# Retention heads of a decoder trunk: the transposes of a head in one row, and query and key products over two banks

## The chip, the cores and the metric

The kernel runs on one core of a Trainium2 chip. The metric is the device time of one execution in microseconds, as the median of several executions. Beside it stands one profiled execution, from which all durations in this document come. Engines are named as in the profile: PE is TensorE (PEld its weight loads), DVE is VectorE, ACT is ScalarE, POOL is GpSimd, SP issues the DMAs.

## The reference

A decoder trunk of two layers, 256 tokens, model width 2048, in float32. Layer 0 mixes tokens by retention, layer 1 by a short gated convolution, and each is followed by a SwiGLU feed-forward stage. The change touches the retention layer alone:

```python
def retention_mixer(h, cos, sin, w_in, w_out):
    q, k, v, g = jnp.split(h @ w_in, [qk_w, 2 * qk_w, 2 * qk_w + v_w], axis=-1)
    q = rope(split_heads(q, RET_HEADS), cos, sin)
    k = rope(split_heads(k, RET_HEADS), cos, sin) * (RET_DK ** -0.5)
    v = split_heads(v, RET_HEADS)
    ...
    o = rms_norm(chunked_gated_linear_attention(q, k, v, log_a))
    o = merge_heads(o).astype(h.dtype)
    return ((jax.nn.silu(g) * o) @ w_out).astype(h.dtype)
```

There are 8 heads; a head has 256 query and key columns and 512 value and gate columns.

## The kernel before, in words

**Products in two parts.** Activations and weights are held as a high part (`hi`, float32r) and a rest (`lo`). A product of a 128x128 weight block with all 256 tokens is hi·h_hi + hi·h_lo + lo·h_hi. There are two ways to write it. `packed` issues three matmuls of 256 columns, all adding into one half of a PSUM bank (L397, L398, L399), so that two blocks of output columns share a bank. `product`, which the feed-forward stages and the output projections use, issues one matmul of 512 columns, whose moving operand is both parts of h and whose results fill a bank (L357), and one of 256 columns for lo, into the second half (L360); its two halves are added later (`summed`: ScalarE copies one, VectorE adds the other, L407 and L409). A value or gate product of width 512 goes by `by_token` (L372 to L374): the tokens are the stationary operand, and a block of 512 columns takes six matmuls. PSUM has eight banks, all from one pool, which hands a bank on when its last reader is through.

**Weights.** They come by DMA in 1 MB tiles in the order of use. Each half of a tile is prepared, two halves ahead, by ScalarE (`hi`, L312) and VectorE (`lo`, L315); a half holds 8 blocks of 128 columns. VectorE also reduces modulation weights (L246) at a lower priority.

**Order.** The instructions of TensorE stand in the order in which the program writes them. Those of VectorE and ScalarE in the heads' stage are ordered by a scheduler's priorities.

**The retention layer.** An opening stage computes, for some heads, the query, key and gate products over part of the 16 rows of weights, and holds the sums in SBUF (`ahead`). Then the heads follow in the order 4, 0, 2, 1, an output projection for these four, 5, 3, 6, 7, and the second output projection. The rows left for the head's own products are none for head 4, four for heads 0 and 1, eight for 2 and 3, and sixteen for 5, 6 and 7. `projections` writes a head as: query product and `rope`, key product and `rope`, value product, scores, gate product. With two blocks of columns each for query and key, all heads together have 2 x 2 x (2 x 4 + 2 x 8 + 3 x 16) = 288 such blocks.

**What a head leaves to the next.** `mixed` returns three steps, which run between the matmuls of whatever follows, after 8, 8 and 20 ticks (a tick is a block of 128 columns): the outputs of the first 128 tokens, those of the second with the norm and the gate (L878, giving the two tiles `o`), and `ends`. `ends` transposes `o` (two tiles of 128x512) into four pieces of 128x256 with eight transposes (L890) and splits each piece into its high and low part, `mid` (L414 on ScalarE, L415 on VectorE). Two pieces share a bank. The program's dependencies go by bank: a write to a bank waits for the reads of it that the program wrote before. `mid` is what the output projection reads; the four pieces of the latest head come last in it.

Of the kernel before, what the change touches and what calls it, by code (L numbers as in the profile page):

```python
# [14 lines left out]
ALU = mybir.AluOpType  # L15
PSUM = bass.MemoryType.PSUM

P = 128
D = 2048
S = 256  # L20
# [105 lines left out]
RET_SPANS, RET_HEADS = ret_in_groups()  # L126
# [61 lines left out]
def trunk(ctx: ExitStack, tc: tile.TileContext, x_in, c_in, pos_in, w_mod, cols_in, tab_in, w_all, out):  # L188
    nc = tc.nc
# [7 lines left out]
    def name(s):  # L197
        serial[0] += 1
        return f"{s}_{serial[0]}"

    def tmp(tag, shape=(P, S), dtype=F32, pool=work, bufs=None):
        return pool.tile(list(shape), dtype, tag=tag, name=name(tag), bufs=bufs)
# [24 lines left out]
    inv_freq, ident = tab[:, 0:1], tab[:, 1 : 1 + P]  # L227
# [107 lines left out]
    def bank():  # L335
        return ps.tile([P, 2, S], F32, tag="bank", name=name("bank"))
# [10 lines left out]
    def product(g, act, base=0, before=None, banks=None, last=True):  # L347

        fresh = not banks
        banks = banks or [bank() for _ in g.cols]  # L350
        for k in g.ks:
            if before:
                before(k)
            h = act[k - base]
            for c, pt in zip(g.cols, banks):
                hi, lo = take(g, k, c)
                nc.tensor.matmul(  # L357
                    pt, hi, h, start=fresh and k == g.ks[0], stop=False, skip_group_check=True
                )
                nc.tensor.matmul(  # L360
                    pt[:, 1, :], lo, h[:, 0, :], start=False, stop=last and k == g.ks[-1], skip_group_check=True
                )
            ticked(len(g.cols))
        paced(len(g.cols) * len(g.ks))
        return banks
# [10 lines left out]
    def packed(g, act, base=0, before=None, between=None, banks=None):  # L376

        banks = banks or [bank() for _ in range((g.n + 1) // 2)]
        for k in g.ks:
            if before:
                before(k)
            h = act[k - base]
            at = 0
            for i, (c, width) in enumerate(g.items):
                if between and i == len(g.items) // 2:
                    between(k)
                hi, lo = take(g, k, c, width)  # L390
                if width == DV:
                    by_token(banks[at // 2 : at // 2 + 2], hi, lo, h, k == g.ks[0], k == g.ks[-1])
                    at += 4
                    continue
                pt = banks[at // 2][:, at % 2, :]
                first, last = k == g.ks[0] and at % 2 == 0, k == g.ks[-1]
                nc.tensor.matmul(pt, hi, h[:, 0, :], start=first, stop=False, skip_group_check=True)  # L397
                nc.tensor.matmul(pt, hi, h[:, 1, :], start=False, stop=False, skip_group_check=True)  # L398
                nc.tensor.matmul(pt, lo, h[:, 0, :], start=False, stop=last, skip_group_check=True)  # L399
                at += 1  # L400
            ticked(g.n)
        paced(g.n * len(g.ks))
        return banks

    def summed(pt, dst=None, at=slice(0, S)):
        low = tmp("low", bufs=3)
        nc.scalar.copy(low[:, at], pt[:, 1, at])  # L407
        dst = tmp("sum", bufs=4) if dst is None else dst
        nc.vector.tensor_tensor(dst, pt[:, 0, at], low[:, at], op=ALU.add)  # L409
        return dst  # L410

    def split(dst, src, at=slice(0, S)):

        nc.scalar.copy(dst[:, 0, at], src)  # L414
        nc.vector.tensor_tensor(dst[:, 1, at], src, dst[:, 0, at].bitcast(F32), op=ALU.subtract)  # L415
# [66 lines left out]
    h = [h_all[:, j, :, :S] for j in range(KT)]  # L482
# [83 lines left out]
    with ExitStack() as inner:  # L566
# [48 lines left out]
        ahead = {}  # L615

        free, tag_of = [f"mid{n}" for n in range(20)], {}
# [13 lines left out]
        with tc.tile_pool(name="start", bufs=1) as sp:  # L631
# [59 lines left out]
            with tc.manual_schedule(engines={mybir.EngineType.DVE, mybir.EngineType.Activation}):  # L691
# [16 lines left out]
                for i in range(0, D, 2 * S):  # L708
                    pt = bank().rearrange("p a b -> p (a b)")
# [24 lines left out]
                pt = norm_sums([acc[0][:, 0, :]])  # L734
# [16 lines left out]
                banks = [bank() for _ in range(8)]  # L751
# [48 lines left out]
        mid = [None] * (4 * HEADS)  # L800

        rp = inner.enter_context(tc.tile_pool(name="rpool", bufs=1))

        def rope(s, tag):
            a = tmp("qa", (P, 2, S), pool=rp, bufs=1)
            nc.vector.tensor_tensor(a, s, cos.unsqueeze(1).to_broadcast([P, 2, S]), op=ALU.mult)
            b = tmp("qb", (P, 2, S), pool=rp, bufs=1)
            nc.vector.tensor_tensor(b[:, 0, :], s[:, 1, :], sin, op=ALU.mult)
            nc.vector.tensor_tensor(b[:, 1, :], s[:, 0, :], sin, op=ALU.mult)
            nc.vector.tensor_tensor(a[:, 0, :], a[:, 0, :], b[:, 0, :], op=ALU.subtract)  # L810
            nc.vector.tensor_tensor(a[:, 1, :], a[:, 1, :], b[:, 1, :], op=ALU.add)
            dst = rp.tile([P, 2, 2, S], F32R, tag=tag, name=name(tag))
            nc.scalar.copy(dst[:, 0, :, :], a)
            nc.vector.tensor_tensor(dst[:, 1, :, :], a, dst[:, 0, :, :].bitcast(F32), op=ALU.subtract)
            return dst

        def gate(s):

            g = rp.tile([P, 2, S], F32, tag="sg", name=name("sg"), bufs=2)
            nc.scalar.activation(g, s, AF.Silu)  # L820
            return g.rearrange("p a b -> p (a b)")
# [34 lines left out]
        def mixed(head, both, v, sg):  # L856

            total = tmp("osum", (P, 2), bufs=2)
            pts, os = [], []

            def outputs(t):

                pt = bank().rearrange("p a b -> p (a b)")
                pts.append(pt)
                n = 0
                for jt in range(t + 1):
                    sp = both[jt][:, :, (t - jt) * P : (t - jt + 1) * P]
                    for i, j in ((0, 0), (0, 1), (1, 0)):
                        nc.tensor.matmul(pt, sp[:, i, :], v[:, jt, j, :], start=n == 0, stop=n == 3 * t + 2)
                        n += 1  # L870
                sq = rp.tile([P, DV], F32, tag="o", name=name("sq"), bufs=2)
                nc.scalar.activation(sq, pt, AF.Square, accum_out=total[:, t : t + 1])

            def normed_outputs():
                r = roots_of(total, DV)
                for t, pt in enumerate(pts):
                    o = rp.tile([P, DV], F32, tag="o", name=name("o"), bufs=2)
                    nc.vector.scalar_tensor_tensor(o, pt, r[:, t : t + 1], sg[t], op0=ALU.mult, op1=ALU.mult)  # L878
                    os.append(o)

            def last_outputs():
                outputs(1)
                normed_outputs()

            def ends():
                for i in range(4):
                    if i % 2 == 0:
                        pt = bank()
                    for t, o in enumerate(os):
                        nc.tensor.transpose(  # L890
                            pt[:, i % 2, t * P : (t + 1) * P], o[:, i * P : (i + 1) * P], ident
                        )
                    n = 4 * head + i
                    mid[n] = rm_tile(("mid", n), F32R)
                    split(mid[n], pt[:, i % 2, :])

            return list(zip(STEPS, [lambda: outputs(0), last_outputs, ends]))

        def pair(head, i):

            g = RET_HEADS[head][0][i]
            if not g.ks:
                return [ahead[head, n] for n in ((i,) if i < 2 else (2, 3))]
            sums = packed(g, h)
            for j, pt in enumerate(sums):
                key = (head, i + j)
                if key in tag_of:
                    free.append(tag_of.pop(key))
                if key in ahead:
                    s = tmp("qs", (P, 2, S), pool=rp, bufs=1)  # L910
                    nc.vector.tensor_tensor(s, ahead[key], pt, op=ALU.add)
                    sums[j] = s
            return sums

        def projections(head):
            q = rope(*pair(head, 0), "q")
            k = rope(*pair(head, 1), "k")
            v = values(head, RET_HEADS[head][1])
            sp = scores(head, q, k)
            sg = [gate(s) for s in pair(head, 2)]  # L920
            asides.extend(mixed(head, sp, v, sg))
            since[0] = 0

# [45 lines left out]
    mid = [mpool.tile([P, 2, S], F32R, tag=f"mid{i}", name=name("mid")) for i in range(KT)]  # L969
    pending, done = [], 0  # L970
    for i, g in enumerate(CONV_IN):
        pending += [sums(g)] if i else normed(acc, 1, 0, g)
        while len(pending) >= 3:
            pb, pc, pu = pending[:3]
            pending = pending[3:]
            j = done
# [74 lines left out]
```

## Time and the profile before

| | us |
|---|---|
| median of three executions | 2684.3 (2682.7 to 2688.4) |
| the profiled execution, its own time | 2684.1 |
| its span, from the first to the last instruction | 2682.3 |
| heads' stage with both output projections | about 195 to 825 of the span |

A row of the waits list reads: engine, tile and line that waited, what ended the wait, then total us, number of waits, the longest. A row of the table by windows gives, for one stretch, the busy time of each engine in us with its instructions, the granted TensorE clock as a share of full speed (PEclk), the busy share of the DMA engines and GB/s. In the timeline a row is one or several equal instructions with start and duration in us; matmuls overlap, so the spacing of their starts, not the duration, is what one costs.

### The profile page before, as it was taken

Reading aid. Unit: us, or ns where it says so; the run is one execution under the profiler, and the core shown is the slowest. Engines: PE = TensorE matmul, PEld = TensorE weight load, DVE = VectorE, ACT = ScalarE, POOL = GpSimd, SP = SyncE. Lnnn points to the kernel's source line nnn. Section 1 sums busy time; section 2 is a strip of 40 time slices with the busy share of each in tenths; the row PEclk is TensorE's granted clock in tenths of the full one; section 3 lists DMA queues with packets and bytes.
Section 4 is the critical chain, followed back from the end, with each engine's and each line's share of the span. In section 5 each row is a group of like instructions: output and inputs, shape, how many; then the busy total and the mean of one; then the engine's idle time right before and its main releaser. Section 6 shows DMA issues by size and latency. Waiting matters only on the chain.

```text
span 2682.3 us, 38239 instructions
## 1 busy us (share of the span) xinstructions
PE 2627.3 (98%) x15220; PEld 2303.8 (86%) x15220; DVE 1993.6 (74%) x2543; ACT 1248.4 (47%) x1770; POOL 145.8 (5%) x230
## 2 busy tenths in 40 slices
PE   7999899999999999999999999999999999999998
PEld 6988789878889888888888898888998888888887
DVE  7997768777678887777777879888886765555564
ACT  5644443444446454334444454444554443444443
POOL 0000000100000001100000001100000000000000
PEclk9999999999999999999999999999999999999999
DMA  9966558866767887777777768776767665555553
GB/s 398 388 269 242 222 192 313 295 226 253 250 223 254 301 307 282 272 279 282 282 273 276 276 221 313 297 281 247 280 252 266 256 230 188 189 189 189 189 189 126
DMA packets 96950, 687.58 MB, mean 256 GB/s; under 512 B 10753, under 2 KB 12545, under 8 KB 13825
## 3 DMA queue, kind: packets, MB, share of 16 engines
q1 hardware_dynamic: 96770, 685.13, 68.8%
q8 instruction: 119, 1.95, 0.3%
q14 instruction: 61, 0.50, 0.0%
HBM read 682.99 MB, written 2.10 MB: 255 GB/s over the span
## 4 chain that ended last, share of the span: by engine, by line
PE 73%; issue 19%; DVE 4%; DMA 2%; ACT 1%; POOL 0%; DVEq 0%; ACTq 0%; POOLq 0%
PE bank L357 34%; PE bank L360 17%; PE bank L372 4%; PE bank L373 4%; PE bank L374 4%; PE bank L399 2%; PE bank L397 2%; PE bank L398 2%; PE bank L517 1%; PE bank L516 1%; PE bank L518 1%; DVE lo L315 1%; DMA raw<-w_all 1%; DVE raw L642 1%; DMA raw<-w_mod 1%
## 5 line engine op out<-in xcount | busy, mean ns | idle before, releaser
L315 DVE TENSOR_TENSOR lo<-raw,hi 128x1024 fp32r<-128x1024 f32 x912 | 1113.5, 1224 | 583.2 <-ACT hi L312 581.1
L312 ACT CAST hi<-raw 128x1024 fp32r<-128x1024 f32 x912 | 955.1, 1052 | 1118.4 <-PE bank L357 644.3
L357 PE MATMUL bank<-h,hi 128*128 128x512 f32 x3296 | 1155.3, 395 | 0.0
L360 PE MATMUL bank<-h,lo 128*128 128x256 f32 x3296 | 924.4, 280 | 0.0
L357 PEld LDWEIGHTS bank<-h,hi 128*128 128x128 f32 x3296 | 622.5, 189 | 145.3
L360 PEld LDWEIGHTS bank<-h,lo 128*128 128x128 f32 x3296 | 622.0, 189 | 0.0
L357 PE MATMUL bank<-mid,hi 128*128 128x512 f32 x1604 | 556.3, 393 | 0.0
L360 PE MATMUL bank<-mid,lo 128*128 128x256 f32 x1604 | 444.9, 277 | 0.1
L246 DVE SCALAR_TENSOR_TENSOR raw<-raw,cb 128x2048 f32<-128x2048 f32 x160 | 365.8, 2286 | 13.7 <-DMA raw<-w_mod 13.5
L357 PEld LDWEIGHTS bank<-mid,hi 128*128 128x128 f32 x1604 | 300.7, 187 | 69.4
L360 PEld LDWEIGHTS bank<-mid,lo 128*128 128x128 f32 x1604 | 301.3, 188 | 0.5 <-DVE lo L315 0.5
L372 PE MATMUL bank<-hi,h 128*128 128x512 f32 x512 | 206.1, 403 | 0.0
L373 PE MATMUL bank<-lo,h 128*128 128x512 f32 x512 | 205.3, 401 | 0.0
L374 PE MATMUL bank<-hi,h 128*128 128x512 f32 x512 | 205.0, 400 | 0.0
L357 PE MATMUL bank<-rm,hi 128*128 128x512 f32 x496 | 177.2, 401 | 0.0
L399 PE MATMUL bank<-h,lo 128*128 128x256 f32 x512 | 147.1, 287 | 6.8 <-DVE lo L315 6.8
L397 PE MATMUL bank<-h,hi 128*128 128x256 f32 x512 | 146.9, 287 | 2.5 <-ACT h L670 2.5
L398 PE MATMUL bank<-h,hi 128*128 128x256 f32 x512 | 146.5, 286 | 0.5 <-DVE h L671 0.5
L360 PE MATMUL bank<-rm,lo 128*128 128x256 f32 x496 | 139.9, 282 | 0.0
L374 PEld LDWEIGHTS bank<-hi,h 128*128 128x128 f32 x512 | 98.4, 192 | 23.4
L372 PEld LDWEIGHTS bank<-hi,h 128*128 128x128 f32 x512 | 98.7, 193 | 20.2
L373 PEld LDWEIGHTS bank<-lo,h 128*128 128x128 f32 x512 | 98.3, 192 | 20.1
(152 smaller groups left out, 2255.3 us busy)
## 6 DMA issues: line engine op xcount, KB each, us to landing
raw<-w_all SPq DMA_DIRECT2D x456, 1024.0 KB, 4.9
raw<-w_mod SPq DMA_DIRECT2D x192, 1024.0 KB, 5.0
x<-x_in SPq DMA_DIRECT2D x4, 512.0 KB, 5.6
out<-out SPq DMA_DIRECT2D x5, 256.0 KB, 2.9
decay<-tab_in SPq DMA_DIRECT2D x8, 128.0 KB, 2.1
out<-out SPq DMA_DIRECT2D x3, 128.0 KB, 2.3
out<-out SPq DMA_DIRECT2D x1, 384.0 KB, 2.7
cols<-cols_in SPq DMA_DIRECT2D x1, 160.0 KB, 8.7
```

Source lines behind the costliest of these rows:

```text
L246: nc.vector.scalar_tensor_tensor(raw, raw, 1.0, cb, op0=ALU.mult, op1=ALU.mult, accum_out=total)
L312: nc.scalar.copy(hi, raw)
L315: nc.vector.tensor_tensor(lo, raw, hi.bitcast(F32), op=ALU.subtract)
L357: nc.tensor.matmul(pt, hi, h, start=fresh and k == g.ks[0], stop=False, skip_group_check=True)
L360: nc.tensor.matmul(pt[:, 1, :], lo, h[:, 0, :], start=False, stop=last and k == g.ks[-1], skip_group_check=True)
L372: nc.tensor.matmul(o, ht[:, 0, :], hi, start=first, stop=False)
L373: nc.tensor.matmul(o, ht[:, 0, :], lo, start=False, stop=False)
L374: nc.tensor.matmul(o, ht[:, 1, :], hi, start=False, stop=last)
L397: nc.tensor.matmul(pt, hi, h[:, 0, :], start=first, stop=False, skip_group_check=True)
L398: nc.tensor.matmul(pt, hi, h[:, 1, :], start=False, stop=False, skip_group_check=True)
L399: nc.tensor.matmul(pt, lo, h[:, 0, :], start=False, stop=last, skip_group_check=True)
L516: nc.tensor.matmul(pt, hi, rows[0], start=k == 0, stop=False)
```

## The change

`ends` takes both banks first, issues the eight transposes in one row, tile by tile of `o`, and then the four splits. The query and key products of a head go through `product` instead of `packed`: a product holds two banks instead of one. Where a partial sum is held, VectorE adds it to the first halves of both banks and then adds the second halves, four operations of 256 columns in place of one of 512; where none is held, `summed` puts the sums into SBUF, and `rope` reads them there instead of from the bank. For head 4, which has no rows left, nothing changes in the products. The gates keep `packed`, in a function of their own.

```diff
             def ends():
+                turned = [bank() for _ in range(2)]
+                for t, o in enumerate(os):
+                    for i in range(4):
+                        nc.tensor.transpose(
+                            turned[i // 2][:, i % 2, t * P : (t + 1) * P], o[:, i * P : (i + 1) * P], ident
+                        )
                 for i in range(4):
-                    if i % 2 == 0:
-                        pt = bank()
-                    for t, o in enumerate(os):
-                        nc.tensor.transpose(
-                            pt[:, i % 2, t * P : (t + 1) * P], o[:, i * P : (i + 1) * P], ident
-                        )
                     n = 4 * head + i
                     mid[n] = rm_tile(("mid", n), F32R)
-                    split(mid[n], pt[:, i % 2, :])
+                    split(mid[n], turned[i // 2][:, i % 2, :])
...
         def pair(head, i):
 
             g = RET_HEADS[head][0][i]
+            key = head, i
             if not g.ks:
-                return [ahead[head, n] for n in ((i,) if i < 2 else (2, 3))]
-            sums = packed(g, h)
-            for j, pt in enumerate(sums):
-                key = (head, i + j)
-                if key in tag_of:
+                return ahead[key]
+            banks = product(g, h)
+            s = tmp("qs", (P, 2, S), pool=rp, bufs=1)
+            if key in ahead:
+                free.append(tag_of.pop(key))
+                for n, pt in enumerate(banks):
+                    nc.vector.tensor_tensor(s[:, n, :], ahead[key][:, n, :], pt[:, 0, :], op=ALU.add)
+                for n, pt in enumerate(banks):
+                    nc.vector.tensor_tensor(s[:, n, :], s[:, n, :], pt[:, 1, :], op=ALU.add)
+            else:
+                for n, pt in enumerate(banks):
+                    summed(pt, s[:, n, :])
+            return s
...
         def projections(head):
-            q = rope(*pair(head, 0), "q")
-            k = rope(*pair(head, 1), "k")
+            q = rope(pair(head, 0), "q")
+            k = rope(pair(head, 1), "k")
             v = values(head, RET_HEADS[head][1])
             sp = scores(head, q, k)
-            sg = [gate(s) for s in pair(head, 2)]
+            sg = gates(head)
```

More of the change, by code (lines that the diff above doesn't have):

```diff
@@ L901, in pair, with gates @@
             g = RET_HEADS[head][0][i]
+            key = head, i
             if not g.ks:
-                return [ahead[head, n] for n in ((i,) if i < 2 else (2, 3))]
-            sums = packed(g, h)
-            for j, pt in enumerate(sums):
-                key = (head, i + j)
-                if key in tag_of:
+                return ahead[key]
[11 more added lines that the diff above has]
+            return s
+        def gates(head):
+            g = RET_HEADS[head][0][2]
+            if not g.ks:
+                return [gate(ahead[head, n]) for n in (2, 3)]
+            sg = []
+            for t, pt in enumerate(packed(g, h)):
+                key = (head, 2 + t)
+                if key in ahead:
                     free.append(tag_of.pop(key))
-                if key in ahead:
                     s = tmp("qs", (P, 2, S), pool=rp, bufs=1)
                     nc.vector.tensor_tensor(s, ahead[key], pt, op=ALU.add)
-                    sums[j] = s
-            return sums
+                    pt = s
+                sg.append(gate(pt))
+            return sg
         def projections(head):
-            q = rope(*pair(head, 0), "q")
-            k = rope(*pair(head, 1), "k")
+            q = rope(pair(head, 0), "q")
+            k = rope(pair(head, 1), "k")
             v = values(head, RET_HEADS[head][1])
             sp = scores(head, q, k)
-            sg = [gate(s) for s in pair(head, 2)]
+            sg = gates(head)
             asides.extend(mixed(head, sp, v, sg))
```

## The prediction

> **What bounds the kernel now.** I read the page first, then the waits of the matmul engine, then its timeline around one place, then stretches in the table by windows.
>
> ```profile
> span 2682.3 us, 38239 instructions
> PE 2627.3 (98%) x15220; PEld 2303.8 (86%) x15220; DVE 1993.6 (74%) x2543; ACT 1248.4 (47%) x1770; POOL 145.8 (5%) x230
> ```
>
> TensorE (PE) is busy 98% of the span, so the time is the length of its instruction stream plus its waits. Its own waits:
>
> ```profile
> PE bank L890 <- DVE rm L415: 26.3, 16, 2.5
> PE bank L399 <- DVE lo L315: 6.8, 6, 2.3
> ```
>
> The first row is by far the largest: 26.3 us in 16 waits, all before a transpose (L890) and all ended by VectorE's half of a split (L415). Eight heads give 16, two for each head. The second row lies in the opening stage, which the change leaves alone. One head's transposes, as TensorE ran them:
>
> ```profile
> 229.81 0.39 PE L373 MATMUL bank<-lo,h 128*128 128x512 f32 x1
> 230.04 0.39 PE L374 MATMUL bank<-hi,h 128*128 128x512 f32 x1
> 230.27 0.38 PE L890 MATMUL bank<-tab,o 128*128 128x128 f32 x2
> 232.50 0.66 PE L890 MATMUL bank<-tab,o 128*128 128x128 f32 x4 [1.85 <-DVE rm L415]
> 234.30 0.69 PE L890 MATMUL bank<-tab,o 128*128 128x128 f32 x2 [1.14 <-DVE rm L415]
> 234.64 0.78 PE L372 MATMUL bank<-hi,h 128*128 128x512 f32 x1
> 235.21 0.63 PE L373 MATMUL bank<-lo,h 128*128 128x512 f32 x1
> 235.64 0.63 PE L374 MATMUL bank<-hi,h 128*128 128x512 f32 x1
> 236.06 0.63 PE L372 MATMUL bank<-hi,h 128*128 128x512 f32 x1
> 236.49 0.63 PE L373 MATMUL bank<-lo,h 128*128 128x512 f32 x1
> 236.92 0.63 PE L374 MATMUL bank<-hi,h 128*128 128x512 f32 x1
> ```
>
> Columns are start, duration, engine, line, operands, and the idle time before. Two transposes run, the next two wait 1.85 us because they write the bank that the split of the first two is still reading, then four run (the third pair is in a fresh bank), and the last two wait 1.14 us for the split of the third pair. Behind them the 512-column matmuls start 0.43 us apart (235.64, 236.06, 236.49, 236.92), where before the transposes they started 0.23 us apart (229.81, 230.04). So the wait has a second price, the granted clock:
>
> ```profile
> core 0: us, PE busy (x) PEld busy (x) DVE busy (x) ACT busy (x) POOL busy (x), PEclk, DMA share, GB/s
> 234.04:237.45 3.41, 3.15 (x9) 2.57 (x10) 0.63 (x2) 0.37 (x1) 0.00 (x0) 0.50 0.82 271
> ...
> 752.86:756.27 3.41, 3.41 (x13) 2.82 (x12) 1.68 (x2) 0.10 (x1) 0.00 (x0) 0.50 0.40 166
> sum 27.28, PE 26.16 PEld 22.55 DVE 15.47 ACT 4.77 POOL 0.69; mean PE 3.27 PEld 2.82 DVE 1.93 ACT 0.60 POOL 0.09
> ```
>
> These are eight stretches of 3.41 us, one behind each head's transposes, all at a clock of 0.50, with 26.16 us of busy TensorE in them. What brings such a stretch is seen in the ones just ahead, cut at the same 3.41 us steps:
>
> ```profile
> 36.07:39.48 3.41, 3.41 (x23) 3.07 (x21) 3.41 (x3) 0.17 (x1) 0.00 (x0) 1.00 1.00 408
> 32.66:36.07 3.41, 2.26 (x16) 2.06 (x16) 3.03 (x4) 3.38 (x6) 0.00 (x0) 1.00 1.01 418
> 152.12:155.53 3.41, 1.49 (x12) 1.48 (x12) 3.41 (x6) 3.21 (x5) 0.00 (x0) 1.00 0.10 38
> 155.53:158.94 3.41, 3.41 (x12) 2.86 (x11) 3.41 (x4) 1.05 (x2) 0.00 (x0) 0.50 0.95 387
> 230.63:234.04 3.41, 0.68 (x5) 0.42 (x4) 3.41 (x6) 1.31 (x4) 0.00 (x0) 1.00 0.01 2
> ```
>
> After 2.26 us busy out of 3.41 the next stretch keeps the full clock; after 1.49 (no transposes in it) and after 0.68 (transposes) the next has half. The point lies between 1.49 and 2.26.
>
> **The change part by part. First, the transposes in a row.** Both banks are taken before the first transpose and all four pieces of a bank are written before its split starts, so neither of the two waits has anything left to wait for: 26.3 us go. A wait also breaks the overlap of neighbours:
>
> ```profile
> L890 PEld LDWEIGHTS bank<-tab,o x64: 137/141/226, 230.0 to 752.2; 128*128 128x128 f32 x64
> L890 PE MATMUL bank<-tab,o x64: 270/272/476, 230.3 to 752.3; 128*128 128x128 f32 x64
> ```
>
> A transpose lasts 0.272 us alone but follows its neighbour after one weight load, 0.141 us, so each of the 16 waits costs another 0.131 us that its idle column does not show: 2.1 us. Sum 28.4 us. Check on the head shown: 234.64 − 230.27 = 4.37 us, less 8 × 0.141 = 1.13, is 3.24; its two waits give 1.85 + 1.14 + 2 × 0.131 = 3.25.
>
> The four splits (eight instructions, as before) now follow with no transpose queued behind them. Only the output projection reads their results, and that comes after four heads; the last head of each four has its transposes inside that projection, whose own rows for this head are kept for last. So they cost TensorE nothing while VectorE finds the time.
>
> **Second, the clock.** With the stalls gone a 3.41 us stretch holds 1.13 us of transposes and matmuls otherwise, so it is busy throughout. A 512-column matmul takes 0.233 us at the full clock and 0.427 at half; the 26.16 busy us shrink by 1 − 0.233/0.427 = 0.454, which is 11.9 us. Bounds: 0, if something else keeps the clock low, and 8 × 3.41 × 0.454 = 12.4.
>
> On this the Trainium skill speaks against the change: "TensorE: Matmul & The Clock Gate", Part 4, says that transpose-mode work does not count as busy for the clock. By it the eight transposes would be 1.13 us of idle to the clock, which alone leaves 2.28 counted; no run here has transposes back to back, so the trace neither bears it out nor refutes it. The sum by the rule is the same unless another wait comes beside them (a rival below).
>
> **Third, query and key products.** Three 256-column matmuls for a weight block (L397 to L399) become one of 512 and one of 256 columns (L357, L360): the same 768 columns, one instruction and one weight load less. Rates from long stretches, by starts:
>
> ```profile
> 453.83 0.28 PE L397 MATMUL bank<-h,hi 128*128 128x256 f32 x1
> ...
> 476.67 0.39 PE L372 MATMUL bank<-hi,h 128*128 128x512 f32 x1
> ```
> ```profile
> 366.94 0.39 PE L357 MATMUL bank<-rm,hi 128*128 128x512 f32 x1
> ...
> 375.41 0.38 PE L890 MATMUL bank<-tab,o 128*128 128x128 f32 x2
> ```
>
> The first is head 5's 64 blocks: 22.84/64 = 0.357 us. The second is 24 blocks of an output projection: 8.47/24 = 0.353. A row of the groups from 195 to 770 us counts the blocks:
>
> ```profile
> L397 PE MATMUL bank<-h,hi 128*128 128x256 f32 x288 | 82.5, 286 | 0.0
> ```
>
> 288 × 0.004 = 1.2 us saved; bounds 0 and 2.4. The durations (three of 0.286 against 0.40 + 0.28) promise far more, but matmuls overlap and only starts count.
>
> **Fourth, VectorE has more to do.** Four heads add their held partial sums: one 512-column add (0.68 us) for each product becomes four of 256. Three heads fed rope from the bank: now ScalarE copies two 256-column halves and VectorE adds two. What these cost:
>
> ```profile
> L911 DVE TENSOR_TENSOR qs<-rm,bank 128x512 f32<-128x512 f32 x16 | 10.9, 682 | 0.8 <-PE bank L399 0.8
> L407 ACT COPY low<-bank 128x256 f32<-128x256 f32 x8 | 3.1, 382 | 0.1
> 229.61 0.42 DVE L810 TENSOR_TENSOR qa<-qa,qb 128x256 f32<-128x256 f32 x1
> 229.95 0.42 DVE L811 TENSOR_TENSOR qa<-qa,qb 128x256 f32<-128x256 f32 x1
> ```
>
> A 256-column operation starts 0.34 us after another, so a product costs about 4 × 0.34 − 0.6 = 0.76 us more in the first case and 0.68 in the second: 1.5 us a head. Over a whole head there is room, but not in the short stretch from the query product to the last transpose in the two heads with four rows left (0 and 1):
>
> ```profile
> 215.50:258.10 42.60, 39.61 (x195) 32.99 (x195) 33.60 (x53) 19.92 (x33) 3.50 (x3) 0.96 0.63 226
> 215.51:234.64 19.13, 16.14 (x98) 13.95 (x97) 17.84 (x33) 10.36 (x19) 2.20 (x1) 0.98 0.60 219
> 313.30:332.75 19.45, 15.94 (x96) 13.74 (x95) 16.12 (x28) 9.62 (x16) 0.73 (x1) 1.00 0.55 207
> ```
>
> The fourth column is VectorE: 33.60 us in 42.60 for the head, but 17.84 in the 19.13 us of the stretch. Without the stalls TensorE crosses it in 19.13 − 3.2 = 15.9 us, and VectorE has 17.84 + 1.5 = 19.3 us of work, of which the four splits (4 × 0.42 = 1.7) may come later: 17.6 us, a lack of 1.7. In the second such head it is 16.12 + 1.5 − 1.7 = 15.9 against some 16: none. The weight halves (L315) stand in the same queue, so the lack would show as matmuls of the value product waiting for `lo`. Bounds are 0, because prepared halves cover it, and 19.3 − 15.9 = 3.4 if the splits go first; two heads make 0 to 6.8, and I take the middle, 3.4 us. The other heads' products are two to eight times as long, which gives VectorE the time. The scores need q and k only after the value product, 64 blocks or 22 us later, which hides the longer chain.
>
> **Sum.** 28.4 + 11.9 + 1.2 − 3.4 = 38.1 us. The profiled execution took 2684.1 us (span 2682.3 and 1.8 around it), which is the median of the runs shown, 2684.3, within 0.2. 2684.1 − 38.1 = 2646.0.
>
> **The rivals.**
> - The half clock stays at the heads where VectorE is late. There a stretch could hold 1.13 us of transposes and a wait of 1.7: if transposes count, 1.7 us busy, between the two points above; by the skill's rule 0.6, well under. Two heads cost 2 × 3.41 × 0.454 = 3.1 us: 2649. If back-to-back transposes alone brought it in all eight, 11.9 come back: 2658. Against it: 1.13 of 3.41 leaves 2.28, as much as the stretch that kept the clock.
> - VectorE becomes the bound through all six heads that are followed by another head's products: the 3.4 us bound each, 20.4 in place of 3.4, 2663. For: 17.84 of 19.13. Against: the other stretches hold modulation work that can move.
> - Slower than before: the bank ring. A query or key product now holds two of eight banks, and holds them until the last of two to four VectorE operations; with two output banks, two value banks and the two of the transposes, TensorE could wait for a bank at each of the 14 such products. That decides from 38.1/14 = 2.7 us per product; at 3 us it is 2688. Against: in this stage the waits list shows no bank but L890's, and the sums free a product's banks while TensorE is in the next product.
> - The change doesn't do what it says: the transposes still wait, now before the first of them, for the normed rows. With eight waits of 2 us the clock stays low too, and 28.4 − 16 + 1.2 − 3.4 = 10.2 us are left: 2674. Against: all 16 waits now end on a split, none on those rows.
>
> **How the numbers follow.** The forecast, 2646, has 0.78 with its own bounds: 2641 with no new wait and a larger gain in the products, 2650 with the full new waits. The clock rival has 0.11, VectorE as the bound 0.06, unchanged waits 0.03, the ring 0.02. The range 2640 to 2656 leaves out the last three and the eight-head clock. A measurement of this kernel can tell 0.2%, 5.4 us, from no change; all but the ring lie far beyond it: faster 0.97, same 0.01, slower 0.02.
>
> **What would show it.** Right: no wait of TensorE on the splits, eight transposes within about 1.2 us, clock 1.00 behind them, L357 and L360 with 288 blocks more. If L373 waits for `lo` appear, in heads 0 and 1, the fourth step is sized by them. Wrong: stretches at 0.50 behind the transposes, or waits at the first matmul of a product.

## The result and the profile after

| | before | after |
|---|---|---|
| median, us | 2684.0 (4 runs) | 2646.7 (4 runs) |
| ratio | | 0.9861, 95% interval 0.9845 to 0.9877 |
| profiled execution, own time, us | 2684.1 | 2646.1 |
| its span, us | 2682.3 | 2643.4 |

1.4% faster; the forecast was 2646.0, in 2640 to 2656. The page of the changed kernel, its first lines:

```profile
span 2643.4 us, 37703 instructions
PE 2611.9 (99%) x14932; PEld 2279.7 (86%) x14932; DVE 2000.8 (76%) x2579; ACT 1250.7 (47%) x1782; POOL 147.7 (6%) x230
```

VectorE's busy time has risen by 7 us and TensorE's has fallen by 15. Where the time went is seen in the table by windows over the heads' stage, from the first scores to the feed-forward stage behind the second output projection; first before, then after (columns: stretch, length, busy us of PE, PEld, DVE, ACT, POOL with their instructions, granted clock, DMA share, GB/s):

```profile
214.39:827.51 613.12, 586.86 (x3210) 505.75 (x3208) 462.64 (x599) 263.62 (x363) 41.26 (x72) 0.98 0.68 249
```
```profile
214.10:788.91 574.81, 572.42 (x2921) 482.50 (x2920) 470.85 (x635) 266.49 (x375) 45.07 (x72) 1.00 0.72 266
```

The stage is 38.3 us shorter, of 38.9 in the span. TensorE was idle for 26.3 us of it (613.12 − 586.86) and is now for 2.4; the other 14.4 us are busy time, and the clock column, 0.98 before and 1.00 after, says that most of that was slow work. The waits of TensorE, restricted to 195 to 800 us, have one row left:

```profile
PE bank L373 <- DVE lo L315: 2.4, 2, 1.2
```

The 16 waits of the transposes are gone, and two new ones have come, of the value products for `lo`. The same place as before, at the transposes of the first head:

```profile
228.57 0.39 PE L372 MATMUL bank<-hi,h 128*128 128x512 f32 x1
230.13 0.50 PE L373 MATMUL bank<-lo,h 128*128 128x512 f32 x1 [1.18 <-DVE lo L315]
230.47 0.40 PE L374 MATMUL bank<-hi,h 128*128 128x512 f32 x1
...
231.40 1.03 PE L889 MATMUL bank<-tab,o 128*128 128x128 f32 x8
232.19 0.48 PE L372 MATMUL bank<-hi,h 128*128 128x512 f32 x1
232.51 0.39 PE L373 MATMUL bank<-lo,h 128*128 128x512 f32 x1
232.74 0.39 PE L374 MATMUL bank<-hi,h 128*128 128x512 f32 x1
```

Eight transposes take 0.79 us from their first start to the next matmul (4.37 before), and the matmuls behind them start 0.23 us apart, not 0.43. A wait of 1.18 us stands ahead of them, and it does not bring the clock down. The table by windows, in the steps of 3.41 us of this execution:

```profile
226.66:230.08 3.42, 2.30 (x10) 1.51 (x9) 3.42 (x9) 1.69 (x3) 0.00 (x0) 1.00 0.12 50
230.08:233.49 3.41, 3.36 (x19) 2.88 (x20) 3.41 (x6) 1.12 (x4) 0.00 (x0) 1.00 0.32 74
```

2.30 us of the first step are busy, and the next keeps the full clock. The other wait, in head 1, leaves 2.20 us of its step busy, and there too the clock stays:

```profile
315.43:318.84 3.41, 2.20 (x10) 1.50 (x9) 3.41 (x7) 1.57 (x2) 0.00 (x0) 1.00 0.00 0
318.84:322.26 3.42, 3.42 (x20) 2.89 (x19) 3.42 (x5) 1.43 (x4) 0.00 (x0) 1.00 0.38 115
```

### The profile page after: what moved, and what is told of

Same layout as the page of the kernel before. It is cut to its first block, busy times and chain, and to the rows that moved or that the text cites. A ratio compares the mean times of both kernels' runs of the same rounds, so it can differ in the third digit from the quotient of the medians.

```text
span 2643.4 us, 37703 instructions
## 1 busy us (share of the span) xinstructions
PE 2611.9 (99%) x14932; PEld 2279.7 (86%) x14932; DVE 2000.8 (76%) x2579; ACT 1250.7 (47%) x1782; POOL 147.7 (6%) x230
## 4 chain that ended last, share of the span: by engine, by line
PE 73%; issue 20%; DVE 3%; DMA 2%; ACT 1%; POOL 0%; DVEq 0%; ACTq 0%; POOLq 0%
PE bank L357 37%; PE bank L360 19%; PE bank L373 3%; PE bank L374 3%; PE bank L372 3%; DMA raw<-w_all 2%; PE bank L517 1%; PE bank L516 1%; PE bank L518 1%; DVE raw L642 1%; DMA raw<-w_mod 1%; DVE lo L315 1%; PE bank L399 1%; PE bank L397 1%; PE bank L398 1%
## 5 line engine op out<-in xcount | busy, mean ns | idle before, releaser
L315 DVE TENSOR_TENSOR lo<-raw,hi 128x1024 fp32r<-128x1024 f32 x912 | 1111.5, 1222 | 546.4 <-ACT hi L312 541.5
L357 PE MATMUL bank<-h,hi 128*128 128x512 f32 x3584 | 1257.9, 395 | 0.0
L360 PE MATMUL bank<-h,lo 128*128 128x256 f32 x3584 | 1005.4, 281 | 0.0
L357 PEld LDWEIGHTS bank<-h,hi 128*128 128x128 f32 x3584 | 677.0, 189 | 158.0
L360 PEld LDWEIGHTS bank<-h,lo 128*128 128x128 f32 x3584 | 676.5, 189 | 0.6
L357 PE MATMUL bank<-mid,hi 128*128 128x512 f32 x1604 | 556.3, 393 | 0.0
L360 PE MATMUL bank<-mid,lo 128*128 128x256 f32 x1604 | 444.3, 277 | 0.0
L357 PEld LDWEIGHTS bank<-mid,hi 128*128 128x128 f32 x1604 | 300.8, 188 | 69.9
L360 PEld LDWEIGHTS bank<-mid,lo 128*128 128x128 f32 x1604 | 301.0, 188 | 0.0
L373 PE MATMUL bank<-lo,h 128*128 128x512 f32 x512 | 203.2, 397 | 2.4 <-DVE lo L315 2.4
L357 PE MATMUL bank<-rm,hi 128*128 128x512 f32 x496 | 175.6, 399 | 0.0
L360 PE MATMUL bank<-rm,lo 128*128 128x256 f32 x496 | 139.3, 281 | 0.0
L373 PEld LDWEIGHTS bank<-lo,h 128*128 128x128 f32 x512 | 97.1, 190 | 23.3 <-DVE lo L315 3.8
L357 PEld LDWEIGHTS bank<-rm,hi 128*128 128x128 f32 x496 | 93.2, 188 | 22.9
L360 PEld LDWEIGHTS bank<-rm,lo 128*128 128x128 f32 x496 | 93.7, 189 | 0.3
L407 ACT COPY low<-bank 128x256 f32<-128x256 f32 x234 | 84.7, 364 | 19.3 <-PE bank L360 18.4
```

What stands on the lines that cost most here:

```text
L315: nc.vector.tensor_tensor(lo, raw, hi.bitcast(F32), op=ALU.subtract)
L357: nc.tensor.matmul(pt, hi, h, start=fresh and k == g.ks[0], stop=False, skip_group_check=True)
L360: nc.tensor.matmul(pt[:, 1, :], lo, h[:, 0, :], start=False, stop=last and k == g.ks[-1], skip_group_check=True)
L373: nc.tensor.matmul(o, ht[:, 0, :], lo, start=False, stop=False)
```

## The experiments

Seven runs beside the result. The first four ran on one chip, against 2685.5 us for the kernel before; the other three against 2683.8.

**The changed kernel again**, as the base on that chip.

> The changed kernel once more, on the chip of the next three, so that differences of a few us can be read: 2646, with TensorE waiting twice for lo at L373 (2.4 us in all) and no wait at a transpose. Both theories say the same here; it is their common base.

Measured: 2646.6 us, ratio 0.9852 (0.9834 to 0.987); L373 waits 2.4 us, in two waits.

**The row alone.** `ends` as changed, the query and key products as before (shown against the changed kernel, shortened):

```diff
         def pair(head, i):
             g = RET_HEADS[head][0][i]
...
-            banks = product(g, h)
+            sums = packed(g, h)
...
```

> The eight transposes in a row, query and key products as before (three matmuls of 256 columns, one bank). Theory of the prediction: the row carries everything, the waits (36.6 us of transposes to 6.3) and the clock (no stretch at 0.50 behind them); VectorE has less to do, so the two waits for lo at L373 (2.7 us by starts) are gone too, and the products cost 0.7 to 1.2 us more: 2643 to 2645, 2 us below the changed kernel. Rival: the two-bank products share in the gain, because they free the clock or the banks: then this stays 5 us or more above the changed kernel, 2652 or over.

Measured: 2644.6 us, ratio 0.9843 (0.9824 to 0.9861). The heads' stage:

```profile
214.62:786.11 571.49, 571.49 (x3210) 496.12 (x3209) 460.07 (x599) 262.15 (x363) 46.44 (x71) 1.00 0.74 267
```

TensorE is busy for all of it. So the row carries the gain, waits and clock, and the two-bank products have no share in either. In the medians the row alone is 2.0 us below the changed kernel, which their intervals cannot separate; in the traces its stage is 3.3 us shorter (571.5 against 574.8; 574.6 in the repeat). Summed by starts, the two-bank products gain 1.2 us in the products themselves (101.8 against 103.1) and lose 3.1 in the value and gate products (260.0 against 256.9), where the two waits lie. Another 1.4 us is in the output projections, of which more at the end.

**The two-bank products alone.** `ends` as before, the products as changed (against the changed kernel):

```diff
             def ends():
-                turned = [bank() for _ in range(2)]
-                for t, o in enumerate(os):
-                    for i in range(4):
-                        nc.tensor.transpose(
-                            turned[i // 2][:, i % 2, t * P : (t + 1) * P], o[:, i * P : (i + 1) * P], ident
-                        )
                 for i in range(4):
+                    if i % 2 == 0:
+                        pt = bank()
+                    for t, o in enumerate(os):
+                        nc.tensor.transpose(
+                            pt[:, i % 2, t * P : (t + 1) * P], o[:, i * P : (i + 1) * P], ident
+                        )
...
```

> The two-bank query and key products, with the transposes in pairs as before. Theory of the prediction: the products give 1.2 us; VectorE's extra adds stand ahead of the splits for which the transposes wait, so the 16 waits grow by some 0.3 us each, 26.3 to 31 us, and the half clock stays at all eight places: 2684 to 2692, no faster than before. Rival (the two-bank form shares in the gain): 2675 to 2680.

Measured: 2691.3 us, ratio 1.0024 (1.0011 to 1.0036): slower. Its waits:

```profile
PE bank L890 <- DVE rm L415: 30.9, 16, 5.7
...
PE bank L373 <- DVE lo L315: 1.9, 2, 1.2
```

31 us were expected. The clock is not as expected: twelve steps of 3.41 us at 0.50 instead of eight, at seven places instead of eight. At four of them a second or third slow step follows the first. There the waits reach into the slow step, and even 2.50 us busy in it did not end it:

```profile
756.22:759.64 3.42, 2.50 (x11) 1.91 (x10) 1.27 (x3) 1.12 (x3) 0.00 (x0) 0.50 0.89 297
759.64:763.05 3.41, 3.41 (x12) 2.88 (x11) 2.30 (x2) 0.00 (x0) 0.16 (x1) 0.50 0.03 12
```

The extra adds stand in VectorE's queue. Ahead of the split that ends the longest wait (5.7 us) its timeline has the short adds of the key product, the rest of `rope` and a weight half, where the kernel before had that split right behind the one add of 512 columns. What waits for VectorE at that moment pays: the transposes here, and the value product, here (1.9 us) as in the changed kernel.

**Packed products for the heads with held sums.** The changed kernel, with two banks for heads 5, 6 and 7 alone:

```diff
+            if key in ahead:
+                (pt,) = packed(g, h)
+                free.append(tag_of.pop(key))
+                s = tmp("qs", (P, 2, S), pool=rp, bufs=1)
+                nc.vector.tensor_tensor(s, ahead[key], pt, op=ALU.add)
+                return s
             banks = product(g, h)
...
```

> The changed kernel, but heads with a held partial sum (0, 1, 2, 3) keep the packed product and its one add of 512 columns; only heads 5, 6 and 7 use two banks. Theory of the prediction: the waits for lo at L373 came from the four short adds in heads 0 and 1, so they are gone (2.7 us), and of the products' gain two thirds stay: 2643 to 2645, 2 us below the changed kernel and level with the row alone. Rival: those waits come from the four splits that now follow the row, whatever the products: then they stay at 2.4 us and the time is 2646 to 2647.

Measured: 2646.8 us, ratio 0.9851 (0.9833 to 0.9869). The time is a miss: no gain over the changed kernel. The two waits in heads 0 and 1 are gone, as expected; but two others have come, in the value product of head 5. The waits of TensorE from 195 to 800 us:

```profile
PE bank L372 <- ACT hi L312: 0.9, 1, 0.9
PE bank L373 <- DVE lo L315: 0.8, 1, 0.8
```

and what came ahead of them on VectorE and on ScalarE, from the timeline:

```profile
457.31 2.28 DVE L246 SCALAR_TENSOR_TENSOR raw<-raw,cb 128x2048 f32<-128x2048 f32 x1
...
462.67 2.36 DVE L315 TENSOR_TENSOR lo<-raw,hi 128x1024 fp32r<-128x1024 f32 x2 [0.46 <-ACT hi L312]
```
```profile
461.59 2.00 ACT L312 CAST hi<-raw 128x1024 fp32r<-128x1024 f32 x2 [4.84 <-DMA raw<-w_all]
```

ScalarE stood idle for 4.84 us until a weight tile landed; weights and modulation tiles share three buffers, and VectorE was reducing a modulation tile until 459.6. That this buffer delayed the load is inferred, not shown. These waits are not the doing of this edit alone: the next run, with all query and key products packed, has the same two, of 0.3 and 0.8 us, in the value product of head 5. The two waits together left 1.79 us busy in a step, and the next is at half clock:

```profile
461.20:464.61 3.41, 1.79 (x7) 0.96 (x6) 2.95 (x6) 2.52 (x3) 0.00 (x0) 0.99 1.00 406
464.61:468.00 3.39, 3.39 (x10) 2.65 (x9) 3.11 (x4) 1.99 (x2) 0.00 (x0) 0.50 0.88 280
```

**The clock apart from the waits.** The kernel before, with its waits, but with something for TensorE to do in them:

```diff
             def ends():
+                spare = bank()
                 for i in range(4):
                     if i % 2 == 0:
                         pt = bank()
+                    else:
+                        for n in range(16):
+                            nc.tensor.transpose(
+                                spare[:, n // 2 % 2, n % 2 * P : (n % 2 + 1) * P], os[0][:, :P], ident
+                            )
```

> The kernel before, with its waits left in, but 16 more transposes (of the same tile, into a bank that nobody reads) between the two pairs of each bank, where TensorE waits 1.1 to 2.6 us: 16 x 0.099 = 1.6 us of work inside each wait. It takes the clock apart from the waits. If transposes in a row count as work for the clock: no stretch at 0.50 behind the transposes, 12 us saved, 2 us lost where the wait is shorter than the filler: 2674. If they do not count (the rule that the prediction weighed): the eight stretches at 0.50 stay, 2686.

Measured: 2678.4 us, ratio 0.9978 (0.9967 to 0.9989). Stage and waits:

```profile
216.53:824.27 607.74, 600.68 (x3465) 523.85 (x3464) 461.62 (x599) 262.43 (x363) 44.21 (x71) 1.00 0.70 251
```
```profile
PE bank L896 <- DVE rm L415: 5.9, 7, 1.9
```

The clock is 1.00 through the stage. The stage is 5.4 us shorter although transposes and filler now take 42.2 us by starts instead of 36.6; so everything else became 11.0 us faster. Nearly all of that is the clock. Against the row alone, the output projections are 1.3 us faster (at one of two paces, see the end), and the value and gate products 1.6 us slower (258.5 against 256.9), where the two waits in head 5 lie. Of the 10 us that were expected, 4.6 are missing, and 3.6 of these are the filler (5.6 us more than before, not 2). Its transposes start 0.109 us apart and not 0.099, so 16 of them take 1.75 us; by the waits of the kernel before, that is longer than nine of the sixteen, by 4.8 us in all.

**64 transposes in a row.**

```diff
-                for t, o in enumerate(os):
-                    for i in range(4):
...
+                for _ in range(8):
+                    for t, o in enumerate(os):
+                        for i in range(4):
...
```

> The changed kernel with the row of eight transposes issued eight times over, 64 in a row, 6.3 us a head, so that at least one whole step of 3.41 us holds nothing but transposes. If transposes count as work for the clock: 7 x 8 x 0.79 = 44 us more, less 2.7 because VectorE catches up: 2688, clock 1.00 at all eight. If they do not: the clock falls to 0.50 within and behind each row, at least 8 x 1.6 = 12 us more, 2700 or over.

Measured: 2694.9 us, one execution. The timeline at the first head, and the step of 3.41 us that holds only transposes with the one behind it:

```profile
231.69 7.16 PE L890 MATMUL bank<-tab,o 128*128 128x128 f32 x64
238.60 0.48 PE L372 MATMUL bank<-hi,h 128*128 128x512 f32 x1
238.92 0.39 PE L373 MATMUL bank<-lo,h 128*128 128x512 f32 x1
```
```profile
233.61:237.02 3.41, 3.41 (x33) 3.41 (x32) 0.76 (x1) 0.00 (x0) 0.00 (x0) 1.00 0.99 360
237.02:240.43 3.41, 3.41 (x25) 3.10 (x24) 0.93 (x3) 1.45 (x5) 0.00 (x0) 1.00 0.48 204
```

No half clock, here or at any other head. These transposes, which the profile lists as MATMUL without saying in which mode they ran, count as work for the clock. The rule of the Trainium skill that the prediction weighed ("TensorE: Matmul & The Clock Gate", Part 4) does not hold for them. The time is 7 us over the expected 2688. 5 of these are in the transposes, 49.0 us more in all and not 44: they start 0.108 us apart, and the 0.79 us of a row of eight are seven such steps and only 0.03 us from the last to the matmul behind. The waits for `lo` did not go either, 1.8 us in two: one of 1.3 in head 0, ahead of the row, and one of 0.6 in head 5; the one in head 1 is gone.

**One bank for all eight.** Four transposes, their two splits, then the other four into the same bank:

```diff
-                turned = [bank() for _ in range(2)]
...
+                turned = bank()
+                for i in range(4):
+                    for t, o in enumerate(os):
                         nc.tensor.transpose(
+                            turned[:, i % 2, t * P : (t + 1) * P], o[:, i * P : (i + 1) * P], ident
                         )
...
+                    if i % 2:
+                        for m in (i - 1, i):
...
+                            split(mid[n], turned[:, m % 2, :])
```

> The changed kernel with four transposes in a row, their two splits, and then the other four into the same bank: one wait a head in place of none (changed) or two (before). If the wait on the bank's readers is what the change removed: a wait of 3 us or more in each of the eight heads (both splits of the first half, with the weight halves between them), and with it the half clock behind each: 24 us or more and 12, 2682 or over. If it is the order alone that matters, four in a row instead of pairs: half of the gain stays, 2665.

Measured: 2692.5 us, one execution, with this row first in its waits:

```profile
PE bank L889 <- DVE rm L415: 32.4, 8, 8.3
```

One wait a head costs as much as two did: 32.4 us against 30.9 in the two-bank products alone, which has the same products. Both splits must end, and weight halves stand between them: in the longest wait, which ends at 547.80, VectorE starts one split at 545.87, a weight half (L315) at 546.20 and the other split at 547.33. Eleven steps of 3.41 us are at 0.50. In this one execution the row of four is worth nothing by itself; what pays is that no transpose follows a read of its bank.

## Why the prediction was right

**The waits.** 28.4 us were forecast, 30.3 came: the transposes went from 36.6 to 6.3 us by starts. The step counted 0.141 us for a transpose in a row, the time of a weight load; in the trace they start 0.109 us apart. With that, a wait costs 0.272 − 0.109 = 0.163 us beyond its idle column and not 0.131, which makes 26.3 + 16 x 0.163 = 28.9. The other 1.4 us were in transposes that did not wait: in the pairs of the kernel before they started 0.13 us apart on average, and seven of the 64 ran at the half clock, three of them 0.27 us apart.

**The clock.** 11.9 forecast. The row alone makes all but the transposes 11.4 us faster (576.5 to 565.1 us), the filler 11.0, with the transposes still held up by the splits. That separates the two prices of the stalls: 30 us for waiting and 11 for what follows. In one point the step was lucky. It took the steps around the row to be busy throughout; the new waits for `lo` left 2.30 and 2.20 us busy in two of them. The kernel before kept its clock after 1.80 us busy and lost it after 1.60, so by these figures 0.4 to 0.7 us more of waiting would have brought the slow step back at these two heads.

**The products.** 1.2 forecast, 1.2 measured against the row alone. Counting starts and not durations was what kept this term small.

**VectorE.** 3.4 us of new waits forecast, the middle between 0 and 6.8; the profile has 2.4 us of idle time, and the value products lost 3.1. The place (L373 for `lo`, in heads 0 and 1) came as described, but that the size came out is in part luck: by the working it was 1.7 and 0 us, in the trace it is two waits of about 1.2. VectorE's queue ahead of the wait in head 0, which ends at 230.13:

```profile
224.94 1.41 DVE L878 SCALAR_TENSOR_TENSOR o<-bank,rs,sg 128x512 f32<-128x512 f32 x2 [0.49 <-POOL rs L447]
226.26 0.74 DVE L912 TENSOR_TENSOR qs<-qs,bank 128x256 f32<-128x256 f32 x2
...
228.86 2.35 DVE L315 TENSOR_TENSOR lo<-raw,hi 128x1024 fp32r<-128x1024 f32 x2
```

From 224.94 on VectorE has no pause; two of the short adds (L912) and the `rope` of the key stand ahead of the weight half. In head 0 this wait is in all five runs whose products use two banks there, and in none of the four whose products are packed. So the two-bank form brings it; no run tells its short adds from the rest of that form. Head 1 is less clear: its wait is in the changed kernel and the repeat, and not in three other runs with the same products. And waits of 0.3 to 0.9 us in head 5 come in four runs, with the filler too, whose products are packed; there the prediction had seen time enough.

**What was not in the sum** is 1.4 us that the output projections lose against the row alone (175.2 and 173.9 by starts). With it the stage closes: 30.3 for the transposes, 11.4 clock and 1.2 products, less 3.1 and 1.4, make 38.4, against 613.1 − 574.8 = 38.3. That the forecast of 38.1 came so near is partly luck: 1.9 us too little for the waits stand against 0.5 too much for the clock and the 1.4 left out.

**The rivals.** The half clock behind the row, by VectorE's lateness or by the transposes themselves: none of it in the changed kernel. That late operands can bring it is seen in the run with packed products, in a value product. VectorE as the bound in all six heads: no, two heads only. The bank ring: no wait at a first matmul of a product. Waits moved to the front of the row: none.

## What to carry to other kernels

When one engine writes pieces into a shared bank that another reads piece by piece, write all pieces first, into banks taken beforehand; here that was worth 30 us of waiting. Price a stall of TensorE twice, the wait and the slow step behind it, and read the second from the clock column in steps of 3.41 us. A change made of two edits can hide that one of them costs: on their own, one made this kernel 1.6% faster and the other 0.24% slower.

## What the runs showed of the hardware

The clock falls for one step of 3.41 us after a step in which TensorE was busy for too little of it; the step need not be idle. In the heads' stage of all traces it fell after 1.60 us busy and less, and in one run after 1.79; it stayed after 1.80 and more, and in one run after 1.67. So the limit lies at about half a step, and the busy time of the profile does not give it exactly. Before, around 275 us:

```profile
271.58:274.99 3.41, 1.80 (x10) 1.25 (x8) 3.41 (x4) 1.43 (x2) 0.19 (x1) 1.00 0.76 250
274.99:278.41 3.42, 0.79 (x5) 0.56 (x6) 3.40 (x10) 1.27 (x3) 0.00 (x0) 1.00 0.86 314
```

The way back asks for more: a step at 0.50 with 2.50 or 2.61 us busy was followed by another (two-bank products alone, one bank), one with 2.98 us was not (before).

The same two-bank block (L357 and L360) runs at one of two steady paces, 0.3467 or 0.3533 us. In an output projection the pace is the same in all runs up to the transposes of the last head (0.353 just ahead of them), and one of the two from there to its end, 207 blocks in the first projection. The first projection has the faster pace before, in the row alone and with packed heads, and the slower one in the changed kernel and its repeat; the second has the slower one in all of these, but the faster one with the filler and with 64 transposes. Over 207 blocks that is 1.4 us, the loss that the prediction's sum lacked. No run here tells what sets it.
